# Low part of split weights in the second mixer: scaled ScalarE copy and an adding GpSimd transfer in place of a VectorE subtraction

## The chip, the cores and the metric

The kernel runs on one core of one Trainium2 chip. The metric is the device time of one execution in microseconds, the median of several runs. A profile is one execution of the same program, recorded by the hardware profiler.

## The reference

A trunk of two layers on a sequence of 256 tokens with 2048 features, all in float32. Each layer is a root-mean-square norm, a token mixer and a residual add, then a norm, a gated feed-forward block (5504 hidden features, a depthwise convolution of width 3 on the gate branch) and a residual add. The first layer's mixer is a bidirectional mLSTM with 8 heads. The second one's, which the change touches, is a bidirectional gated linear recurrence (HGRN2) with 16 heads of 128:

```python
p = hn @ w_in                       # 2048 -> 3*2048 + 2*2048
q, i, g, f_f, f_b = split(p)
k, log_f = gate(f)                  # for f_f and f_b; lower bound lb
y = hgrn_direction(q, k_f, lf_f, v) + flip(hgrn_direction(flip(q), flip(k_b), flip(lf_b), flip(v)))
y = head_rmsnorm(y, head_g, B_HEADS) * silu(g)
return y @ w_out
```

What the change touches is how the weights of `hn @ w_in` are prepared.

## The kernel before

**Big products.** All matrix products with weights are one stream. A Chunk is a block of output columns over all k-tiles of 128: kind "fm" (256 columns, features on the partitions), "tm" (512 columns, tokens on the partitions) or "one". `stream` takes the chunks in order and issues TensorE's matmuls (L181 to L183 for "tm", L188 and L189 for "fm").

**Split weights.** TensorE multiplies in the type float32r, which holds fewer bits than float32. `split_weights` therefore makes of each weight two float32r parts whose sum is the weight. SyncE loads up to 2048 columns (1 MiB) into a `raw` buffer (L133; three buffers, `RAW`). Then for each piece of 1024 columns ScalarE casts `raw` to the high part `wh` (L139), and VectorE subtracts `wh` from `raw` to give the low part `wl` (L140). `wh` and `wl` have four buffers each (`WB`), and `stream` fetches three pieces ahead of their use (`LOOK`). A "tm" piece is two k-tiles with 12 matmuls of 512 columns (high x high, high x low, low x high for two halves of the tokens). An "fm" piece is four k-tiles with 16 matmuls: for each of two blocks of features `wh` times both parts of x (512 columns), and `wl` times the high part (256 columns).

**The second mixer.** `hgrn` lays out its input products in four rounds, each for four heads: one "tm" chunk of `w_bv` (8 pieces), six "fm" chunks of `w_bq` (24 pieces; q, forward gate and backward gate of the heads), one "tm" chunk of `w_bg` (8 pieces). 160 pieces in all. When a chunk of `w_bq` is done, `take` evicts it (ScalarE copy L200, VectorE L201, L206), makes the gates (ScalarE L548, L549; VectorE L550, L551) and the products with q on GpSimd (L552, L554, L557). The head's own chain is then fed into the stream as side work: for seven levels, small matmuls `pd` (L590), VectorE products `QK` (L591, L592), copies `km` and `qm` (L574), masked copies into `AT` (L569), and GpSimd products `G` (L597). Matmuls `py` (L613) end it. The output projection `w_bout` follows, with the same split of its weights.

**The order.** The program text gives an order by `side.tick`, which counts assumed product time. A scheduler then fixes the order of instructions on each engine when the program is built. Each engine works through its own list in that order; GpSimd issues its transfers from the same list as its arithmetic, and SyncE issues the weight loads.

Of the kernel before, what the change touches and what calls it, by code (L numbers as in the profile page):

```python
# [8 lines left out]
F32 = mybir.dt.float32  # L9
F32R = mybir.dt.float32r  # L10
I32 = mybir.dt.int32
AF = mybir.ActivationFunctionType
ALU = mybir.AluOpType
# [3 lines left out]
T = 256  # L17
D = 2048
KT = D // P
# [21 lines left out]
LOOK = 3  # L41
# [9 lines left out]
def trunk_kernel(ctx, tc, xT, pp_d, cst_d, w_gate, w_aq, w_ak, w_av, w_ao, w_aout,  # L51
                 w_bq, w_bv, w_bg, w_bout, w_up, w_down, out, mscr, stop=9):
    nc = tc.nc
    act, dve, pool, pe = nc.scalar, nc.vector, nc.gpsimd, nc.tensor
# [13 lines left out]
    hT = [hx[:, k] for k in range(KT)]  # L68
# [6 lines left out]
    def aux(name):  # L75
        return psa.tile([P, 512], F32, tag="aux", name=name)

# [1 line left out]
    class Side:  # L79
        def __init__(self):  # L80
            self.now, self.jobs = 0.0, []
# [24 lines left out]

    side = Side()

# [1 line left out]
    class Chunk:  # L110
        def __init__(self, kind, src, nk, x, done, before=None, last=False):
            self.last = last
            self.kind, self.src, self.nk, self.x, self.done, self.before = kind, src, nk, x, done, before
            self.width = {"fm": 256, "tm": 512, "one": P}[kind]

    def split_weights(chunks):
        """raw -> the exact sum of two float32r parts, LOOK pieces ahead of their use"""
        first = True
        for ch in chunks:
            total = ch.nk * ch.width  # L120
            cuts = [0, 512, 1024] if first else [0]
            if ch.last and total % 1024:
                cuts.append(total % 1024)
            while cuts[-1] < total:
                cuts.append(min(total, cuts[-1] + (1024 if first else 2048)))
            for b0, b1 in zip(cuts, cuts[1:]):
                n = b1 - b0
                if first:
                    for k0, k1 in {0: [(0, 1)], 512: [(1, 2)], 1024: [(2, 4)], 2048: [(4, 8)], 4096: [(8, 12)],
                                   6144: [(12, 16)]}.get(b0, []):  # L130
                        nc.sync.dma_start(hx[:, k0:k1], xT[:, k0:k1])
                raw = wpool.tile([P, 2048], F32, tag="raw", bufs=RAW, name="raw")
                nc.sync.dma_start(raw[:, :n], ch.src[:, b0:b0 + n])  # L133
                for c0 in range(0, n, 1024):
                    m = min(1024, n - c0)
                    wh = wpool.tile([P, 1024], F32R, tag="wh", bufs=WB, name="wh")
                    wl = wpool.tile([P, 1024], F32R, tag="wl", bufs=WB, name="wl")
                    r = raw[:, c0:c0 + m]
                    act.copy(wh[:, :m], r)  # L139
                    dve.tensor_tensor(wl[:, :m], r, wh[:, :m].bitcast(F32), ALU.subtract)  # L140
                    yield wh, wl, m // ch.width
            first = False

    def stream(chunks):
        pieces = split_weights(chunks)
        ready = []

# [62 lines left out]
    def late(dst, src):  # L210
        tc.keep_in_program_order(nc.sync.dma_start(dst, src))

# [1 line left out]
    class Norm:  # L214
        def __init__(self, gname, goff, final=False, first=False):
            self.first = first
# [52 lines left out]
        return rs  # L269

    def project(wsrc, nk, x, norm):
        """hT += W^T x, 256 features at a time; the next norm takes each tile as it is done."""
        def done(c):
            def f_(ps):
                for f in range(2):
                    k = 2 * c + f
                    if norm is not None and norm.final and c == 7:
                        dve.tensor_tensor(hT[k], hT[k], ps[f][:, 0:T], ALU.add)
                        norm.add(k)
                        continue  # L280
                    b = ev.tile([P, T], F32, tag="b", bufs=3, name="b")
                    act.copy(b, ps[f][:, T:2 * T])
                    dve.tensor_tensor(hT[k], hT[k], ps[f][:, 0:T], ALU.add)
                    dve.tensor_tensor(hT[k], hT[k], b, ALU.add)  # L284
                    if norm is not None:
                        norm.add(k)
            return f_
        return [Chunk("fm", wsrc(c), nk, x, done(c), last=(norm is not None and norm.final and c == 7))
                for c in range(8)]
# [2 lines left out]
        where = keep if j < KT else more  # L292
        return where.tile([P, 2 * T], F32R, tag=f"yt{j}", name=f"{name}{j}")

# [1 line left out]
    def mlstm(norm, nxt):  # L296
        YT = [None] * KT
        H = 64
# [191 lines left out]
        def end():  # L490
            side.drain()
            stack.close()

        tail = project(lambda c: w_aout[c], KT, yx, nxt)
        tail[1].before = end
        return chunks + tail

# [1 line left out]
    def hgrn(norm, nxt):  # L499
        YT = [None] * KT  # L500
        stack = ExitStack()
# [118 lines left out]
        def finish(qd, four):  # L620
            for j in range(4):
                hd = 4 * qd + j
                while "y" not in heads[hd]:
                    yield
                y, rs = heads[hd]["y"]
                for t in range(2):
                    c = slice(t * P, (t + 1) * P)
                    dve.scalar_tensor_tensor(y[:, c], y[:, c], rs[:, t:t + 1], four["sg"][:, t, j * P:(j + 1) * P],
                                             ALU.mult, ALU.mult)
                yield  # L630
                pz = aux("pz")
                for t in range(2):
                    c = slice(t * P, (t + 1) * P)
                    pe.transpose(pz[:, c], y[:, c], ident)
                YT[hd] = slot(hd, "yb")
                split(YT[hd], pz[:, 0:T], col("b_head_g", hd))

        heads = [dict() for _ in range(BH)]
        chunks = []
        for qd in range(BH // 4):  # L640
            four = dict()

            def done_v(ps, four=four):
                four["V"] = box["mp"].tile([P, 2, 512], F32, tag="V", bufs=1, name="V")
                for t in range(2):
                    act.activation(four["V"][:, t], ps[t], AF.Copy, scale=norm.rc[:, t:t + 1])

            def done_g(ps, four=four, qd=qd):
                sg = four["sg"] = box["mp"].tile([P, 2, 512], F32, tag="sg", bufs=1, name="sg")
                for t in range(2):  # L650
                    act.activation(sg[:, t], ps[t], AF.Sigmoid, scale=norm.rc[:, t:t + 1])
                    dve.scalar_tensor_tensor(sg[:, t], ps[t], norm.rc[:, t:t + 1], sg[:, t], ALU.mult, ALU.mult)
                side.push(finish(qd, four))

            chunks.append(Chunk("tm", w_bv[qd], KT, norm.x, done_v, begin if qd == 0 else None))
            for i in range(6):
                def done_i(ps, i=i, qd=qd):
                    for f in range(2):
                        r = 2 * i + f
                        take(4 * qd + r // 3, r % 3, ps[f])  # L660
                chunks.append(Chunk("fm", w_bq[6 * qd + i], KT, norm.x, done_i))
            for j in range(4):
                heads[4 * qd + j]["qd"] = four
            chunks.append(Chunk("tm", w_bg[qd], KT, norm.x, done_g))

        def yx(k):
            side.until(lambda: YT[k] is not None)
# [2 lines left out]
        def end():  # L670
            side.drain()
            stack.close()

        tail = project(lambda c: w_bout[c], KT, yx, nxt)
        tail[1].before = end
        return chunks + tail

# [1 line left out]
    def ffn(layer, norm, nxt):  # L679
        stack = ExitStack()  # L680
        box = {}
# [25 lines left out]
        for part, (f0, nf) in enumerate(((0, FA), (FA, FB))):  # L707
            GT = []
            for i in range(nf):
                chunks.append(Chunk("fm", w_up[layer, f0 + i], KT, norm.x, done_up(f0 + i, i, GT),  # L710
                                    begin if f0 + i == 0 else None))
            chunks += project(lambda c: w_down[layer, c][:, f0 * 256:(f0 + nf) * 256], nf,
                              lambda k, GT=GT: GT[k], nxt if part else None)
        return chunks, stack.close

# [1 line left out]
    pool.memset(ones, 1.0)  # L717
    pool.memset(hmx, -0.5)
    pool.memset(pad, 0.0)
# [6 lines left out]
    chunks = mlstm(n0, n1)  # L726
# [17 lines left out]
    if stop > 3:  # L744
        order = ((0, pool), (2, dve), (3, dve), (1, pool), (4, dve), (5, dve), (6, dve), (7, dve))
        for n, (c, eng) in enumerate(order):
            r = (nf.R if eng is pool else nf.pr[:, 0:T]).unsqueeze(1).broadcast_to([P, 2, T])
# [8 lines left out]


def _cols(w, width):
    """[K, n*width] -> [n, 128, (K/128)*width]: a chunk of columns, its k-tiles side by side on each partition."""
    K, N = w.shape  # L760
    v = w.reshape(K // P, P, N // width, width).transpose(2, 1, 0, 3)
    return np.ascontiguousarray(v).reshape(N // width, P, (K // P) * width)


def _pcol(v):
    """[..., n*128] -> [128, ...*n]"""
    return np.asarray(v).reshape(-1, P).T


# [63 lines left out]
```

## Time and profile before

| | us |
|---|---|
| median of 3 runs | 2487.5 |
| lowest and highest run | 2486.99, 2487.65 |
| span of the profiled execution, first to last instruction | 2485.1 |
| busy in the span: TensorE matmul, VectorE, ScalarE, GpSimd | 2453.6, 1799.6, 1195.9, 311.0 |

For the profiled execution only its span is recorded; the runs' median lies 2.4 us above it. In the profile PE is TensorE's matmuls, PEld its weight loads, DVE VectorE, ACT ScalarE, POOL GpSimd, SP SyncE. L140 is line 140 of the kernel. A group's row gives line, engine, operation, output <- inputs, shapes and count, then busy us and mean ns of one, then the idle time of the engine just before these instructions and what ended it. A row of a DMA issue ends with KB of one and median us from issue to landing. "Landing" is when all of a transfer has arrived.

### The profile page before, as it was taken

Reading aid. Unit: us, or ns where it says so; the run is one execution under the profiler, and the core shown is the slowest. Engines: PE = TensorE matmul, PEld = TensorE weight load, DVE = VectorE, ACT = ScalarE, POOL = GpSimd, SP = SyncE. Lnnn points to the kernel's source line nnn. Section 1 sums busy time; section 2 is a strip of 40 time slices with the busy share of each in tenths; the row PEclk is TensorE's granted clock in tenths of the full one; section 3 lists DMA queues with packets and bytes.
Section 4 is the critical chain, followed back from the end, with each engine's and each line's share of the span. In section 5 each row is a group of like instructions: output and inputs, shape, how many; then the busy total and the mean of one; then the engine's idle time right before and its main releaser. Section 6 shows DMA issues by size and latency. Waiting matters only on the chain.

```text
span 2485.1 us, 35987 instructions
## 1 busy us (share of the span) xinstructions
PE 2453.6 (99%) x13934; PEld 2138.7 (86%) x13934; DVE 1799.6 (72%) x3001; ACT 1195.9 (48%) x1802; POOL 311.0 (13%) x368
## 2 busy tenths in 40 slices
PE   8999999999999999999999999999999999999998
PEld 6888888888888888888888888888888888888887
DVE  7766677777656777666979798897777765677754
ACT  5555455544444444444444444445544444444543
POOL 4100032000000000121404131324000000000022
PEclk9999999999999999999999999999999999999999
DMA  6654555555556555556454544545556555665553
GB/s 240 190 178 165 187 178 188 193 187 188 186 189 199 187 188 190 185 187 195 147 170 137 169 153 153 166 140 187 187 186 189 193 184 192 192 189 190 190 189 123
DMA packets 66204, 449.07 MB, mean 181 GB/s; under 512 B 7649, under 2 KB 8161, under 8 KB 15729
## 3 DMA queue, kind: packets, MB, share of 16 engines
q1 hardware_dynamic: 64656, 443.56, 54.8%
q0 software_dynamic: 800, 2.16, 0.6%
q8 instruction: 109, 1.79, 0.3%
q10 hardware_dynamic: 576, 1.05, 0.1%
q14 instruction: 63, 0.51, 0.1%
HBM read 444.58 MB, written 2.16 MB: 180 GB/s over the span
## 4 chain that ended last, share of the span: by engine, by line
PE 89%; DVE 8%; issue 2%; ACT 0%; DMA 0%; SPq 0%; DVEq 0%; POOL 0%; POOLq 0%
PE mm L188 49%; PE mm L189 25%; PE mm L182 4%; PE mm L183 4%; PE mm L181 4%; DVE wl L140 3%; DVE QK L591 1%; DVE AT L569 1%; PE pd L590 1%; DVE QK L592 1%; DVE qm L574 1%; DVE km L574 1%; PE pn L408 1%; PE mm L170 1%; PE py L613 0%
## 5 line engine op out<-in xcount | busy, mean ns | idle before, releaser
L140 DVE TENSOR_TENSOR wl<-raw,wh 128x1024 fp32r<-128x1024 f32 (+2 forms) x859 | 1051.8, 1225 | 550.2 <-ACT wh L139 536.9
L188 PE MATMUL mm<-xt,wh 128*128 128x512 f32 x3792 | 1324.5, 394 | 0.0
L139 ACT CAST wh<-raw 128x1024 fp32r<-128x1024 f32 (+2 forms) x859 | 884.2, 1030 | 857.8 <-PE mm L188 475.6
L189 PE MATMUL mm<-xt,wl 128*128 128x256 f32 x3792 | 1060.4, 280 | 0.0
L188 PEld LDWEIGHTS mm<-xt,wh 128*128 128x128 f32 x3792 | 710.7, 187 | 160.6
L189 PEld LDWEIGHTS mm<-xt,wl 128*128 128x128 f32 x3792 | 715.0, 189 | 0.4
L188 PE MATMUL mm<-g,wh 128*128 128x512 f32 x1334 | 462.6, 392 | 0.0
L189 PE MATMUL mm<-g,wl 128*128 128x256 f32 x1334 | 371.6, 279 | 0.0
L188 PEld LDWEIGHTS mm<-g,wh 128*128 128x128 f32 x1334 | 249.8, 187 | 56.3
L189 PEld LDWEIGHTS mm<-g,wl 128*128 128x128 f32 x1334 | 251.3, 188 | 0.0
L181 PE MATMUL mm<-wh,xt 128*128 128x512 f32 x512 | 203.3, 400 | 6.1 <-ACT wh L139 6.1
L182 PE MATMUL mm<-wl,xt 128*128 128x512 f32 x512 | 204.5, 399 | 4.6 <-DVE wl L140 4.6
L183 PE MATMUL mm<-wh,xt 128*128 128x512 f32 x512 | 202.7, 396 | 0.0
L200 ACT COPY b<-mm 128x256 f32<-128x256 f32 x237 | 87.6, 370 | 180.7 <-PE mm L189 180.7
L232 POOL TENSOR_TENSOR acc<-hx 128x256 f32<-128x256 f32 x5 | 5.4, 1085 | 1242.3 <-DVE hx L284 1239.9
L181 PEld LDWEIGHTS mm<-wh,xt 128*128 128x128 f32 x512 | 97.1, 190 | 26.8 <-ACT wh L139 7.1
L182 PEld LDWEIGHTS mm<-wl,xt 128*128 128x128 f32 x512 | 97.4, 190 | 24.3 <-DVE wl L140 5.9
L183 PEld LDWEIGHTS mm<-wh,xt 128*128 128x128 f32 x512 | 97.4, 190 | 19.5
L235 POOL TENSOR_TENSOR sq<-hx 128x256 f32<-128x256 f32 x65 | 71.7, 1114 | 198.0 <-DVE hx L284 195.5
L188 PE MATMUL mm<-yb,wh 128*128 128x512 f32 x256 | 90.6, 399 | 0.0
L188 PE MATMUL mm<-ya,wh 128*128 128x512 f32 x256 | 89.1, 394 | 0.0
L201 DVE TENSOR_TENSOR a<-mm,b 128x256 f32<-128x256 f32 x86 | 36.5, 424 | 51.0 <-ACT b L200 50.9
(175 smaller groups left out, 2093.2 us busy)
## 6 DMA issues: line engine op xcount, KB each, us to landing
raw<-in_w_up SPq DMA_DIRECT2D x172, 1024.0 KB, 5.1
raw<-in_w_down SPq DMA_DIRECT2D x64, 1024.0 KB, 4.9
raw<-in_w_bq SPq DMA_DIRECT2D x48, 1024.0 KB, 5.1
raw<-in_w_ao SPq DMA_DIRECT2D x16, 1024.0 KB, 4.9
raw<-in_w_aout SPq DMA_DIRECT2D x16, 1024.0 KB, 5.1
raw<-in_w_bv SPq DMA_DIRECT2D x16, 1024.0 KB, 4.9
raw<-in_w_bg SPq DMA_DIRECT2D x16, 1024.0 KB, 4.8
raw<-in_w_bout SPq DMA_DIRECT2D x16, 1024.0 KB, 5.1
```

The lines of the kernel that those rows point to most:

```text
L139: act.copy(wh[:, :m], r)
L140: dve.tensor_tensor(wl[:, :m], r, wh[:, :m].bitcast(F32), ALU.subtract)
L170: pe.matmul(ps[f][:, 0:T], w[:, c:c + P], x[:, o:o + T], start=(k + kk == 0 and i == 0), stop=(k + kk == ch.nk - 1 and i == 2))
L181: pe.matmul(ps[t], xh, wh[:, c], start=st, stop=False)
L182: pe.matmul(ps[t], xh, wl[:, c], start=False, stop=False)
L183: pe.matmul(ps[t], xl, wh[:, c], start=False, stop=sp)
L188: pe.matmul(ps[f], wh[:, c:c + P], x, start=st, stop=False)
L189: pe.matmul(ps[f][:, 0:T], wl[:, c:c + P], x[:, 0:T], start=False, stop=sp)
L200: act.copy(b, ps[:, T:2 * T])
L201: dve.tensor_tensor(dst, ps[:, 0:T], b, ALU.add)
L235: eng.tensor_tensor(s, hT[k], hT[k], ALU.mult)
L574: dve.tensor_copy(m.rearrange("k (m p j) -> k m p j", p=2, j=h), blocks(z, h, 0, T))
```

## The change

For the chunks of `w_bv`, `w_bq` and `w_bg` (marked `summed`), and only for these, the low part is made in another way. ScalarE copies `raw` a second time, with scale -1, into the float32r buffer `wl`, which then holds the negated high part. GpSimd then issues a transfer that reads the same weights once more from HBM and adds them onto `wl`. The sum is the low part. The VectorE subtraction of these 160 pieces is gone. All other weights keep the subtraction. Line numbers from L143 on are four higher in the changed kernel.

```diff
     class Chunk:
-        def __init__(self, kind, src, nk, x, done, before=None, last=False):
-            self.last = last
+        def __init__(self, kind, src, nk, x, done, before=None, last=False, summed=False):
+            self.last, self.summed = last, summed
...
                     act.copy(wh[:, :m], r)
-                    dve.tensor_tensor(wl[:, :m], r, wh[:, :m].bitcast(F32), ALU.subtract)
+                    if ch.summed:
+                        act.activation(wl[:, :m], r, AF.Copy, scale=-1.0)
+                        pool.dma_start(wl[:, :m], ch.src[:, b0 + c0:b0 + c0 + m], accum_op=ALU.add)
+                    else:
+                        dve.tensor_tensor(wl[:, :m], r, wh[:, :m].bitcast(F32), ALU.subtract)
...
-            chunks.append(Chunk("tm", w_bv[qd], KT, norm.x, done_v, begin if qd == 0 else None))
+            chunks.append(Chunk("tm", w_bv[qd], KT, norm.x, done_v, begin if qd == 0 else None, summed=True))
...
-                chunks.append(Chunk("fm", w_bq[6 * qd + i], KT, norm.x, done_i))
+                chunks.append(Chunk("fm", w_bq[6 * qd + i], KT, norm.x, done_i, summed=True))
...
-            chunks.append(Chunk("tm", w_bg[qd], KT, norm.x, done_g))
+            chunks.append(Chunk("tm", w_bg[qd], KT, norm.x, done_g, summed=True))
```

## The prediction

> **What bounds the kernel now.** I read the page first (busy time, chain), then cut the second mixer's input stage into its period and asked for the busy time, the groups and the waits of that stretch.
>
> ```profile
> span 2485.1 us, 35987 instructions
> ...
> PE 2453.6 (99%) x13934; PEld 2138.7 (86%) x13934; DVE 1799.6 (72%) x3001; ACT 1195.9 (48%) x1802; POOL 311.0 (13%) x368
> ...
> PE 89%; DVE 8%; issue 2%; ACT 0%; DMA 0%; SPq 0%; DVEq 0%; POOL 0%; POOLq 0%
> ```
>
> Over the whole span TensorE is the bound: 99% busy, 89% of the chain. VectorE has 8% of the chain. Where the changed pieces are multiplied shows a row of the view of the tile wl, asked for 1107 to 1648 us (durations, first and last start):
>
> ```profile
> L182 PE MATMUL mm<-wl,xt x247: 388/389/486, 1122.6 to 1647.6; 128*128 128x512 f32 x124
> ```
>
> The w_bv and w_bg products on L182 open and close the stage: 1122.6 to 1647.6, 525 us. It is four rounds of 40 pieces (a piece is 1024 columns, 512 KB of weights: 8 for w_bv, 24 for w_bq, 8 for w_bg). Three of the rounds by the view of busy time in given stretches (stretch, length, then busy us of PE, PEld, DVE, ACT and POOL, granted clock, DMA share, GB/s), then a stretch of the first feed-forward stage:
>
> ```profile
> 1198.65:1333.83 135.18, 132.77 (x761) 115.13 (x760) 117.79 (x243) 59.94 (x100) 37.16 (x48) 1.00 0.48 156
> 1333.83:1469.04 135.21, 132.83 (x761) 115.19 (x761) 118.00 (x243) 59.97 (x100) 35.76 (x48) 1.00 0.48 156
> 1469.04:1604.18 135.14, 132.72 (x761) 115.15 (x760) 117.77 (x244) 59.96 (x100) 37.16 (x48) 1.00 0.48 156
> ```
>
> ```profile
> 700.00:1000.00 300.00, 300.00 (x1732) 264.50 (x1732) 203.02 (x310) 142.15 (x200) 0.00 (x0) 1.00 0.59 191
> ```
>
> The reader is to see that a round lasts 135.2 us, so a piece takes 135.2/40 = 3.38 us (3.28 over the 160 of the whole stage, since the first round starts without head work), and that TensorE is idle for only 135.18 - 132.77 = 2.4 us of it although VectorE is at 118 of 135 us. In the same round, the chain by line, one row of its pieces (start, us), the groups of the two engines that make the parts, and the waits (us, times, longest):
>
> ```profile
> by line: DVE wl L140 15.2%; PE mm L188 12.0%; issue 10.0%; DVE QK L591 7.0%; PE mm L182 6.3%; PE mm L181 6.3%; PE mm L183 6.2%; PE mm L189 5.9%; DVE QK L592 5.5%; DVE qm L574 4.6%; DVE AT L569 4.5%; DVE km L574 4.5%; PE pd L590 2.2%; DVE G
> ...
> 1255.12 1.34 PE pd L590 x12
> ```
>
> ```profile
> L140 DVE TENSOR_TENSOR wl<-raw,wh 128x1024 fp32r<-128x1024 f32 x41 | 51.8, 1263 | 14.2 <-ACT wh L139 13.9
> ```
>
> ```profile
> L139 ACT CAST wh<-raw 128x1024 fp32r<-128x1024 f32 x40 | 42.0, 1050 | 32.6 <-PE mm L188 15.0 <-PE mm L183 14.8 <-DVE QK L591 1.2
> ...
> L651 ACT ACTIVATE sg<-mm,rc 128x512 f32<-128x512 f32 x2 | 1.4, 691 | 1.0 <-PE mm L183 1.0
> ```
>
> ```profile
> ACT wh L139 <- PE mm L188: 15.0, 11, 1.8
> ACT wh L139 <- PE mm L183: 14.8, 9, 3.4
> DVE wl L140 <- ACT wh L139: 13.9, 12, 2.1
> ```
>
> Here the subtraction L140 is the largest item of the chain (15.2%), with the heads' VectorE work around it. TensorE and VectorE take turns as the limit. The cast on ScalarE waits mostly for TensorE: it starts when a buffer comes free, so the pipeline already runs at the depth of its four buffers.
>
> **How much there is to win.** The feed-forward stretch has no head work: 1732 matmul rows in 300.0 us, 16 rows a piece, is 300/(1732/16) = 2.77 us a piece. Forty such pieces are 110.8 us. A round has 761 rows, of which 24 x 16 + 16 x 12 = 576 are products; the other 185 belong to the heads, at 1.34/12 = 0.11 us each 20.4 us. TensorE's own work is then 131.2 us of 135.2: 4 us a round, 16 us in four rounds, is all that a free VectorE can give.
>
> **The change part by part.** 160 pieces change (4 x 40). *Removed*: 160 subtractions of 1.26 us on VectorE, 50.5 us a round; VectorE falls to about 67 of 135 us and leaves the chain. By itself: at most -16 us. *ScalarE*: one copy with scale more per piece. The trace has none of that shape. From below it is the cast, 1.05 us; from above 691 ns for 512 columns twice, 1.38 us. I take 1.1, since the cast has the same operands. ScalarE goes from 59.9 to 59.9 + 40 x 1.1 = 104 us of 135: not the bound, but wh and wl of a piece now stand one behind the other, 2.15 us.
>
> *GpSimd*: 160 issues more, each of which waits for ScalarE's copy, and GpSimd takes its work in order. Behind the waiting issue stand the heads' G products (L597), QK products (L552), the copy L554 and the memset L566. VectorE's L591 and L592 wait for G, and TensorE's pd (L590) for those. The issue's own price, and the only transfers that GpSimd makes now:
>
> ```profile
> L380 POOL DMA_DIRECT2D Mb<-mscr x16: 536/546/585, 67.0 to 160.4; - x16
> ...
> DMA to landing us min/median/max: 3.8/5.1/7.2
> ```
>
> Forty issues of 0.55 us are 22 us a round on top of 37: GpSimd has room, 59 of 135. The new order puts the G products one or two between two issues, so a piece that lands late also holds up a head by as much; I count that inside the piece time below, as both follow the same buffer.
>
> *The transfers.* Each adds 512 KB from HBM onto the old content of wl. The rows:
>
> ```profile
> q1 hardware_dynamic: 64656, 443.56, 54.8%
> q0 software_dynamic: 800, 2.16, 0.6%
> ...
> raw<-in_w_bq SPq DMA_DIRECT2D x48, 1024.0 KB, 5.1
> ...
> Mb<-mscr POOLq DMA_DIRECT2D x16, 128.0 KB, 5.1
> ...
> raw<-in_w_down SPq DMA_DIRECT2D x1, 512.0 KB, 3.5
> ```
>
> ```profile
> GB/s 351 150 0 126 384 89 0 206 393 5 0 0 206 393 9 0 103 393 103 0 0 267 332 0 0 178 407 14 9 37 262 300 0 89 384 131 0 0 70 295
> ```
>
> The last row is from the DMA view of 1330 to 1400 us, in slices of 1.75 us: with work queued the 16 engines reach 407 GB/s, so 512 KB (524,288 bytes) passes in 1.29 us. By the share of the first row, 443.56 MB in 54.8% of 2485.1 us is 326 GB/s, 1.61 us. An adding transfer must fetch the old wl as well as the weights before it writes. I found no transfer of that kind in the trace, so its price is bounded: one pass from below (1.29 us, the read of wl costs nothing), two passes of the slow kind from above. That slow kind is q0, the software queue: 2.16 MB in 0.6% of the span, 14.9 us, is 145 GB/s, 3.6 us a pass, 7.2 for two. I take two passes at the speed of the weight loads, because these rows are 4 KB like theirs and the q0 rows are 1 KB.
>
> So a piece now asks the DMA engines for its plain load and two passes more. At 407 GB/s that is 3 x 1.29 = 3.87 us, at 326 GB/s 3 x 1.61 = 4.83 us, and both are over the 3.38 us that a piece takes today. **The DMA engines become the bound of this stage.** With a full queue the 407 is the nearer row; the queue runs empty at times, because a transfer can't start before its buffer is free. I take 4.15 us. By the Trainium skill, Collectives: The Full Stack, section "The bandwidth ceiling: the fold count and why AG ≠ RS ≠ AR", a reducing transfer runs at about half the rate of a copy since it reads two sources, 32.35 against 62.28 GB/s; by that ratio a piece would ask for 1.29 + 1.93 x 1.29 = 3.78 us and the sum would be 2567 us. No run here shows it yet.
>
> *The loop of four buffers.* wl of piece i can be rewritten when TensorE has done with piece i-4, and TensorE wants it three pieces later. In those three piece times must fit: two ScalarE copies 2.15, the issue 0.55, and the time to landing L. With 3 x 3.38 = 10.1 us, L may be 7.4 us before it costs anything. From below L is 3.5 us (512 KB on SyncE's queue), hidden. From GpSimd's queue, 128 KB took 5.1 us; 384 KB more (0.97) and a second pass (1.29) make 7.4, just the cover; with the longest, 7.2, L is 9.5 and a piece (2.7 + 9.5)/3 = 4.05 us. The loop thus has no reserve either, and full DMA engines lengthen L: that is why I stay above 3.87. By the Trainium skill, DMA: Bandwidth & Descriptors, section "Anatomy of one DMA — SWDGE (gpsimd) path", a GpSimd transfer takes 2.0 us plus its bytes at 436 GB/s. That would be 3.2 us for 512 KB and would hide wholly. The trace's Mb row disagrees: 5.1 us for 128 KB, where this rule gives 2.3.
>
> *The rest.* The stages outside keep their instructions; the first pieces are fetched under the end of the feed-forward stage, which moves a few us at most. Sum: the stage goes from 525 to 160 x 4.15 = 664 us, so the span to 2485.1 + 139 = 2624 us. The runs' median, 2487.5, lies 2.4 us above the profiled span, so **2627 us**.
>
> **The rivals.**
> 1. *Faster.* The adding transfer occupies the engines under 3.38 - 1.29 = 2.09 us and lands within 7.4 us. Then VectorE's relief comes through: 2487.5 - 16 = 2472 us. For it: DMA is only 0.48 busy in this stage, and VectorE leads the chain. Against it: two passes (2.58) are already over that point, and only one pass fits.
> 2. *A slow adder.* If the adding queue runs like q0, one pass is 3.6 us and a piece 3.6 + 1.29 = 4.9 us, the stage 784: 2747 us. With two passes 7.2 + 1.61 = 8.8 us, the stage 1408: 3370 us. For it: the only software-queue rows are that slow. Against it: their rows are a quarter as long.
> 3. *Only the loop decides.* The engines keep up but L is 7.4 to 9.5 us: from no loss, 2488 us, to 4.05 us a piece, 2611 us; in the middle 3.6, 2539 us. For it: Mb's 5.1 us. Against it: it needs the cheap pass together with the long landing.
> 4. *Nothing to see*: the relief of VectorE and a small loss cancel, 2483 to 2492 us.
>
> **How the numbers follow.** The forecast, 3.87 to 4.83 us a piece, 2582 to 2735 us: 0.5. Slow adder: 0.2. Loop alone: 0.1. Faster: 0.15. No change: 0.05. About 0.2% (5 us) is what a measurement of this kernel can tell from no change. Faster 0.15, same 0.05, slower 0.80. The range runs from 2470, the full relief, to 2830, a piece of 5.4 us; it leaves out the larger part of the slow adder and hardly anything below.
>
> **What would show it.** In the new profile: rounds of about 166 us instead of 135; DMA share in them near 0.9 or more, not 0.48; TensorE idle some 30 us a round, ended by the landing of wl; VectorE near 67 us and gone from the chain. Loop alone would show the same idle time with a DMA share under 0.8. The slow adder would show wl landings over 12 us. The forecast is wrong if the landings stay under 7.4 us and rounds are shorter than 135 us.

## The result, and the profile after

The changed kernel takes 2563.6 us, the median of 4 runs (2561.58 to 2569.76); the kernel before took 2487.24 us beside it. The ratio is 1.0311, 95% interval 1.0298 to 1.0324: 76 us slower. The profiled execution is the run of 2569.76 us. First lines of its page, and its DMA queues (packets, MB, share of 16 engines):

```profile
span 2568.0 us, 36293 instructions
...
PE 2481.5 (97%) x13934; PEld 2144.6 (84%) x13934; DVE 1646.5 (64%) x2841; ACT 1346.4 (52%) x1962; POOL 408.2 (16%) x528
...
q1 hardware_dynamic: 64656, 443.56, 51.1%
q0 software_dynamic: 23840, 86.06, 17.2%
...
PE 81%; DMA 12%; issue 4%; POOL 2%; ACT 1%; DVE 1%; SPq 0%; DVEq 0%; POOLq 0%; ACTq 0%
```

VectorE fell from 8% of the chain to 1%, and DMA came in with 12%. The stage's ends show best where the output projection (tile yb) begins. Before, then after, the second row of "after" being the first use of wl in the stage:

```profile
L188 PE MATMUL mm<-yb,wh x256: 389/398/481, 1659.4 to 1754.0; 128*128 128x512 f32 x128
```

```profile
L192 PE MATMUL mm<-yb,wh x256: 390/392/477, 1746.0 to 1836.7; 128*128 128x512 f32 x128
```

```profile
L186 PE MATMUL mm<-wl,xt x256: 387/393/628, 1125.3 to 1745.5; 128*128 128x512 f32 x128
```

The stage goes from 1122.6-1659.4, 537 us, to 1125.3-1746.0, 621 us: 84 us more. It starts 2.7 us later, and the projection behind it takes 91 us in place of 95. The sum is the 83 us between the spans. One round after the change, in the columns used above, and the same stretch in the view of DMA queues and issues:

```profile
1319.40:1471.87 152.47, 138.00 (x760) 113.63 (x759) 79.48 (x202) 97.18 (x140) 60.35 (x89) 1.00 1.05 275
```

```profile
DMA  9999999999999999999999999999999999999999
...
q0 software_dynamic: 5732, 20.86, 69.6%
q1 hardware_dynamic: 2873, 20.92, 34.9%
...
wl<-in_w_bq POOLq DMA_DIRECT2D x25, 512.0 KB, 10.0
raw<-in_w_bq SPq DMA_DIRECT2D x12, 1024.0 KB, 9.0
```

The reader is to see four things. The round is 152.5 us, 17 more than before. VectorE is down from 118 to 79 us. The DMA share went from 0.48 to 1.05 (packets of the two queues overlap, hence over 1), and the row of tenths shows 0.9 or more in each of 40 slices. And the plain weight loads, which nobody changed, now land after 9.0 us where they took 5.1.

The two queue rows give the price of the unknown operation. q0: 69.6% of 152.5 us for 20.86 MB is 2.67 us for 512 KB. q1: 34.9% for 20.92 MB is 1.33 us for 512 KB. **In this round an adding transfer keeps the DMA engines busy twice as long as a plain load of the same bytes.** Together 4.0 us of engine time a piece, done in 3.81 (152.5/40) thanks to the overlap. The price of a plain load isn't fixed: before the change 512 KB took 1.61 us (47.3% of the 440 us from 1200 on, 67.95 MB). So a ratio holds only within one stretch.

The waits in the same round, of the copy into wl and of TensorE's weight loads, then those of its matmuls, then the chain:

```profile
ACT wl L141 <- PE mm L186: 15.2, 13, 2.5
...
PEld mm L193 <- DMA wl<-in_w_bq: 13.0, 12, 1.8
```

```profile
PE mm L193 <- DMA wl<-in_w_bq: 9.6, 12, 1.4
PE mm L186 <- DMA wl<-in_w_bv: 3.4, 6, 0.8
PE mm L186 <- DMA wl<-in_w_bg: 1.5, 2, 0.9
```

```profile
by line: DMA wl<-in_w_bq 39.3%; issue 18.7%; DMA wl<-in_w_bg 13.8%; DMA wl<-in_w_bv 7.2%; PE mm L192 5.1%; POOL wl L142 4.6%; PE mm L193 3.8%; ACT wl L141 2.7%; PE pd L594 2.0%; PE mm L186 1.9%; POOL rs L272 1.5%; POOL QK L556 1.5%; PE mm L
```

TensorE waits for landings of wl: the three rows make up all of its 14.5 idle us (152.47 - 138.00), and 60% of the round's chain are these landings. ScalarE waits for TensorE to free wl. Such a ring of waits can't tell by itself whether the slow part is the engines' throughput or the length of the ring. That is what the experiments are for.

### The profile page after: what moved, and what is told of

Read it like the earlier page. It is cut to its first block, busy times and chain, and to the rows that moved or that the text cites. A ratio compares the mean times of both kernels' runs of the same rounds, so it can differ in the third digit from the quotient of the medians.

```text
span 2568.0 us, 36293 instructions
## 1 busy us (share of the span) xinstructions
PE 2481.5 (97%) x13934; PEld 2144.6 (84%) x13934; DVE 1646.5 (64%) x2841; ACT 1346.4 (52%) x1962; POOL 408.2 (16%) x528
## 3 DMA queue, kind: packets, MB, share of 16 engines
q10 hardware_dynamic: 576, 1.05, 0.1%
## 4 chain that ended last, share of the span: by engine, by line
PE 81%; DMA 12%; issue 4%; POOL 2%; ACT 1%; DVE 1%; SPq 0%; DVEq 0%; POOLq 0%; ACTq 0%
PE mm L192 45%; PE mm L193 24%; DMA wl<-in_w_bq 7%; DMA wl<-in_w_bg 3%; PE mm L186 3%; PE mm L187 3%; PE mm L185 3%; DMA wl<-in_w_bv 2%; POOL wl L142 1%; PE pd L594 1%; PE pn L412 1%; ACT wl L141 1%; PE mm L174 1%; PE py L617 0%; DVE xt L200 0%
## 5 line engine op out<-in xcount | busy, mean ns | idle before, releaser
L144 DVE TENSOR_TENSOR wl<-raw,wh 128x1024 fp32r<-128x1024 f32 (+2 forms) x699 | 849.6, 1216 | 497.2 <-ACT wh L139 485.0
L141 ACT ACTIVATE wl<-raw 128x1024 fp32r<-128x1024 f32 x160 | 169.2, 1057 | 62.8 <-PE mm L186 62.4
L142 POOL DMA_DIRECT2D wl<-in_w_bq x96 | 85.0, 887 | 224.5 <-ACT wl L141 145.6
```

What stands on the lines that cost most here:

```text
L141: act.activation(wl[:, :m], r, AF.Copy, scale=-1.0)
L142: pool.dma_start(wl[:, :m], ch.src[:, b0 + c0:b0 + c0 + m], accum_op=ALU.add)
```

## The experiments

Three theories. **A:** the throughput of the DMA engines bounds the stage. **B:** the loop of four buffers bounds it: copy, issue, landing in a row take longer than three pieces of products. **C:** the software queue is slow whatever it carries. The times of the kernel before, in the three groups of runs, were 2487.72, 2487.59 and 2487.39 us.

**The relief alone.** The adding transfer is taken out; wl then holds only the negated high part.

```diff
                         act.activation(wl[:, :m], r, AF.Copy, scale=-1.0)
-                        pool.dma_start(wl[:, :m], ch.src[:, b0 + c0:b0 + c0 + m], accum_op=ALU.add)
```

> The changed kernel without the adding transfers: wl holds the negated high part only (the addition is left out). It shows what VectorE's relief with ScalarE's second copy is worth by itself. Theory A and B: VectorE at about 67 to 80 us of a round, the relief is at most 16 us, time 2471 to 2480 us. If ScalarE's two copies in a row were part of the loss, it would stay above 2487 us.

2472.53 us, ratio 0.9939 (0.9923 to 0.9956), 15 us faster. A round:

```profile
1277.90:1409.60 131.70, 131.70 (x762) 115.12 (x760) 74.07 (x202) 97.44 (x141) 27.29 (x48) 1.00 0.49 160
```

TensorE is busy for all of 131.7 us. ScalarE's double work (97 us) costs nothing. So everything that the change loses, 91 us against this run, comes with the transfers: their engine time, their issues, the waits for them.

**Plain in place of adding.**

```diff
-                        pool.dma_start(wl[:, :m], ch.src[:, b0 + c0:b0 + c0 + m], accum_op=ALU.add)
+                        pool.dma_start(wl[:, :m], ch.src[:, b0 + c0:b0 + c0 + m])
```

> The changed kernel with the adding taken out: GpSimd's 160 transfers are plain copies of the same weights into wl (the low part is then wrong; this leaves out the addition). Same issues, same waits, same bytes from HBM. Theory A (the 16 DMA engines are the bound, an adding transfer costs two passes): a piece asks for 1.36 + 1.36 = 2.7 us instead of 1.36 + 2.65 = 4.0, under the 3.36 us that it takes without the change, so the stage falls from 621 us to 537 or less, time 2470 to 2490 us, DMA share well under 1. Theory B (the loop of four buffers is the bound: copy, issue, landing in a row): the landing shortens by one pass only, 1.3 us in three pieces, stage 552 us or more, time about 2500 us. Theory C (the software queue is slow in itself, whatever it carries): still about 2564 us.

2492.94 us, ratio 1.0023 (1.0014 to 1.0033). A round, and the landings of these transfers (min/median/max):

```profile
1283.90:1421.60 137.70, 134.56 (x762) 116.30 (x761) 75.77 (x202) 97.22 (x141) 48.11 (x88) 0.99 0.89 308
```

```profile
DMA to landing us min/median/max: 3.8/6.0/9.1
```

As many transfers, the same waits and the same HBM bytes without the second pass: 71 us of the loss are gone. C falls. One thing more changed with it: a plain issue takes GpSimd 0.54 us, an adding one 0.88. A piece's transfer now takes 1.58 us of engine time beside 1.45 for a load (46.7% for 71.35 MB and 42.9% for 71.49 MB, of the 460 us from 1140 on). The loads have rows of 8 KB, these transfers of 4 KB; queue and rows together thus cost a tenth, and the rest of the doubling is the adding. But A asked for 2490 at most, and 20 us against the relief alone remain although the engines are no longer full.

**Half of the columns of each piece.**

```diff
-                        pool.dma_start(wl[:, :m], ch.src[:, b0 + c0:b0 + c0 + m], accum_op=ALU.add)
+                        pool.dma_start(wl[:, :m // 2], ch.src[:, b0 + c0:b0 + c0 + m // 2], accum_op=ALU.add)
```

> The changed kernel, but each adding transfer covers only the first 512 of a piece's 1024 columns (the low part of the other half is left wrong). Every piece still goes through copy, issue, landing. Theory A: a piece asks the DMA engines for 1.36 + 1.33 = 2.7 us, no longer the bound, time 2470 to 2490 us. Theory B: the fixed part of the landing and the chain ahead of it stay, the loss falls by less than half, about 2530 us.

2504.89 us, ratio 1.0069 (1.0054 to 1.0084): between the two theories, over A's 2490 and under B's 2530. A round takes 137.6 us with a DMA share of 0.91. Its issues take 0.88 us like those of the change, so the dearer issue can hardly explain more than the 12 us between this run and the plain one.

**Every second piece.**

```diff
-                    if ch.summed:
+                    if ch.summed and c0:
```

> The changed kernel with only every second piece (the second of each 1 MiB load) made by ScalarE and the adding transfer, the first by the VectorE subtraction; nothing is left out. Theory A: 1.36 + 2.65/2 = 2.7 us of DMA engine time a piece, not the bound; VectorE is relieved of half, 25 us a round; time 2474 to 2485 us, faster than the kernel before. Theory B: half of the pieces still pay, about 2520 us.

2508.3 us, ratio 1.0086 (1.0071 to 1.0101). It fails A's expectation, which was faster than before; B's 2520 is nearer. The landings:

```profile
DMA to landing us min/median/max: 5.3/7.9/10.2
```

With half of the load and with all of it, different things seem to rule. The next runs are to part them.

**The load without the loop.** The kernel before, with plain copies whose data nobody waits for.

```diff
                 nc.sync.dma_start(raw[:, :n], ch.src[:, b0:b0 + n])
+                if ch.summed:
+                    late(dscr[turn[0] % 8], ch.src[:, 0:4096])
+                    turn[0] += 1
```

> The kernel before (VectorE subtraction, no adding transfer), but SyncE issues behind each 1 MiB weight load of the second mixer's input products a plain copy of 2 MiB from HBM to an HBM scratch that nobody reads: the DMA engines get as many bytes to pass as the two passes of two adding transfers, and no piece waits for them. Theory A (the DMA engines' throughput bounds the changed stage): the stage goes from 537 to 610 us or more, time 2560 us or more. Theory B (the loop of copy, issue and landing bounds it): about 2488 us, as before.

2615.25 us, ratio 1.0513 (1.0497 to 1.0529). A round of it:

```profile
1318.00:1481.60 163.60, 141.14 (x760) 116.41 (x760) 117.07 (x243) 58.30 (x101) 29.76 (x48) 0.99 0.99 383
```

VectorE still subtracts and no adding transfer is in the way, and the stage is slower than with the change. The weight loads stand behind the copies in SyncE's queue: those of w_bq landed after a median of 18.6 us in place of 5.1, so here the loop of the `raw` buffers grew. But with a DMA share of 0.99 the engines have no time left: engine load alone is enough.

**Finer pieces, all adding.** Pieces of 512 columns with eight buffers, seven ahead, in the same memory.

```diff
-LOOK = 3
+LOOK = 7
-WB = 4
+WB = 8
...
-                for c0 in range(0, n, 1024):
-                    m = min(1024, n - c0)
-                    wh = wpool.tile([P, 1024], F32R, tag="wh", bufs=WB, name="wh")
-                    wl = wpool.tile([P, 1024], F32R, tag="wl", bufs=WB, name="wl")
+                for c0 in range(0, n, 512):
+                    m = min(512, n - c0)
+                    wh = wpool.tile([P, 512], F32R, tag="wh", bufs=WB, name="wh")
+                    wl = wpool.tile([P, 512], F32R, tag="wl", bufs=WB, name="wl")
```

> The changed kernel with pieces of 512 columns in place of 1024 (eight buffers of half the size, seven pieces ahead), in all stages; nothing is left out. In the same memory the cover of the chain grows: seven half pieces are 11.5 us less one copy pair 1.2 and one issue 0.9, 9.4 us, instead of 9.8 - 2.15 - 0.9 = 6.8 us. Theory A: the bytes stay, so the stage stays at 610 to 640 us; the time stays at 2560 us or above. Theory B: the stage falls to 540 us or less, time near that of the kernel before with the same pieces.

2568.94 us, ratio 1.0325 (1.0310 to 1.0341). A round:

```profile
1310.90:1465.30 154.40, 136.96 (x760) 114.21 (x760) 82.57 (x202) 107.81 (x222) 97.45 (x128) 1.00 1.09 273
```

With all the bytes, a longer cover (the time from a buffer's coming free to its next use, less ScalarE's two copies) changes nothing. The landings, of half the bytes each, took a median of 11.7 us, where the same 256 KB took 6.7 in the run with half of the columns: they follow the load of the engines. One reservation: the halved rows take somewhat more engine time by the byte (DMA share 1.09 against 1.05), so a small gain of the loop could hide behind it, not one of 80 us.

**The control for finer pieces**: the kernel before with the same cut.

> The kernel before with pieces of 512 columns in all stages, the control for the two runs with fine pieces. More and shorter instructions on ScalarE and VectorE, no other work: both theories 2485 to 2510 us.

2492.03 us, ratio 1.0018 (1.0009 to 1.0028).

**Finer pieces, every second adding.** The cut above and

```diff
-                    if ch.summed:
+                    if ch.summed and c0 % 1024:
```

> As the run with pieces of 512 columns, but only every second of them is made by the adding transfer; nothing is left out. Half the adding bytes left a loss of about 35 us against the relief alone when the pieces had 1024 columns. If that rest is the loop of buffers (landings of 5.3 to 10.2 us against a cover of 6.8), the cover of 9.4 us takes most of it: 2475 to 2490 us, or 5 to 15 us under the kernel before with the same pieces. If it is the DMA engines' throughput after all, it stays at about 2508 us.

2496.82 us, ratio 1.0037 (1.0023 to 1.0051): 5 us over its control, where the same bytes in coarse pieces stood 21 us over theirs. So with half the load the cover did matter, as B has it. I had expected a win over its control, and there was none. A landing is counted from the start of its issue (in the changed kernel's chain, the landing of 10.34 us from 1319.71 us begins where that issue begins), so the issue must not come off the cover again as it does in the expectation: 11.5 - 1.2 = 10.3 us stand against a median of 7.9 and a longest of 12.8. Cover and size of the transfers changed together here; which of the two brought the 16 us isn't parted.

**One piece in four.**

```diff
-                    if ch.summed:
+                    if ch.summed and c0 and b0 % 4096 == 0:
```

> The changed kernel with one piece in four made by the adding transfer, the others by the subtraction; nothing is left out. Every second piece left 21 us over the kernel before. DMA engine time 1.36 + 0.66 = 2.0 us a piece; VectorE relieved by 12.6 us a round, worth up to 4 us in all. If bursts on the DMA engines make the landings late (theory A with the loop of buffers), fewer adding transfers in a row leave 2485 to 2495 us. If each adding transfer costs a fixed wait, half of the 21 + 8 us: about 2498 us.

2503.59 us, ratio 1.0070 (1.0054 to 1.0087), hardly less than with every second piece. A round, then the landings:

```profile
1291.30:1429.20 137.90, 133.08 (x762) 115.08 (x761) 108.21 (x232) 69.77 (x111) 39.98 (x58) 1.00 0.68 191
```

```profile
DMA to landing us min/median/max: 5.4/8.1/9.3
```

The engines have a third of their time free, and still the landing takes 8.1 us against a cover of 3 x 3.28 - 2.15 = 7.7 us. Here B rules: a typical adding transfer is late by 0.4 us. TensorE's waits for these landings in the whole stage (us, times, longest):

```profile
PE mm L193 <- DMA wl<-in_w_bq: 15.3, 12, 2.0
PE mm L186 <- DMA wl<-in_w_bv: 5.4, 2, 4.9
...
PE mm L186 <- DMA wl<-in_w_bg: 0.6, 1, 0.6
```

That is 21 us in 15 waits for 40 transfers, and the relief of a quarter doesn't pay for it. By engine time an adding transfer costs 2.89 us here and a load 1.62 (21.2% for 17.67 MB, 47.7% for 71.18 MB, of 460 us), a ratio of 1.8.

**Source in SBUF.**

```diff
-                        pool.dma_start(wl[:, :m], ch.src[:, b0 + c0:b0 + c0 + m], accum_op=ALU.add)
+                        pool.dma_start(wl[:, :m], r, accum_op=ALU.add)
```

> The changed kernel, but the adding transfer takes the weights from the raw buffer in SBUF instead of a second time from HBM; nothing is left out. The raw buffer is held until the transfer has landed. Theory A (passes of the DMA engines, whatever the source): two passes remain, stage 610 to 650 us, time 2555 us or more, more if the held raw buffers delay the loads. Rival: the second read of HBM is the price; then the HBM traffic of the stage is as before the change and the time falls under 2520 us.

2600.97 us, ratio 1.0452 (1.0437 to 1.0468). A round lasts 162.5 us with a DMA share of 1.03, and over the 460 us from 1140 on q0 takes 67.5% where q1 takes 35.8% for the same bytes, 1.9 times as much. The second read of HBM isn't the price. That it is even slower than the change fits the raw buffers, which are held longer, but that wasn't tried apart.

**What TensorE waited for.** GpSimd works through its list in order, so an issue that waits for ScalarE also holds up the heads' products behind it. That would be a rival for what remains at part load. The traces answer it: for each run, the median landing and TensorE's matmul waits for landings of wl in the whole stage. The first column is against the kernel before; with 512 columns, against the control.

| GpSimd's transfers | time, us | DMA share of a round | median landing, us | waits for landings, us |
|---|---|---|---|---|
| adding, all pieces (the change) | +76 | 1.05 | 10.3 | 62 |
| adding, source in SBUF | +114 | 1.03 | 9.2 | 77 |
| adding, all, 512 columns | +77 | 1.09 | 11.7 | 63 |
| adding, every second | +21 | 0.87 | 7.9 | 24 |
| adding, half of the columns | +17 | 0.91 | 6.7 | 19 |
| adding, one in four | +16 | 0.68 | 8.1 | 21 |
| adding, every second, 512 columns | +5 | 0.92 | 7.9 | 7 |
| plain, all pieces | +5 | 0.89 | 6.0 | 12 |
| none (relief alone) | -15 | 0.49 | none | 0 |

All other waits of TensorE's matmuls in the stage come to 7 us at most in these runs, and to 10 in the kernel before. So the loss is in the landings, not in heads that GpSimd holds up. A late issue would show as a late landing too; but with one piece in four GpSimd waited ahead of its issues almost only for ScalarE's copy (167 of 168 us). For the change, 62 of the 91 us are such waits; the rest stands in matmul time (138 against 131.7 us a round), whose ends the profile models.

**VectorE relieved without a transfer.** Since the relief was worth 15 us, I moved other VectorE work of this stage to ScalarE, in the kernel before: the copies km and qm.

```diff
-                dve.tensor_copy(m.rearrange("k (m p j) -> k m p j", p=2, j=h), blocks(z, h, 0, T))
+                act.copy(m.rearrange("k (m p j) -> k m p j", p=2, j=h), blocks(z, h, 0, T))
```

> The kernel before with the heads' copies km and qm (56 a round of 0.36 us, 20 us) on ScalarE in place of VectorE; nothing is left out and no transfer is added. The relief alone measured 15 us for 50 us a round less on VectorE. If VectorE's load is what counts, 20 us a round less gives 5 to 10 us: 2478 to 2483 us. If the copies stand behind ScalarE's casts, which wait for buffers, the heads come late and it is slower: 2490 to 2510 us.

2474.02 us, ratio 0.9946 (0.9931 to 0.9961): **faster than both kernels**, 13 us under the kernel before. A round, with all of TensorE's time in use:

```profile
1277.40:1409.20 131.80, 131.80 (x762) 115.21 (x761) 105.73 (x186) 79.84 (x157) 35.65 (x48) 1.00 0.49 160
```

With km alone on ScalarE:

> As the run before it, but only km (28 a round, 10 us) on ScalarE. If VectorE's load counts, 3 to 5 us: 2482 to 2485 us. If the wait behind ScalarE's casts counts, 2488 to 2500 us.

2476.93 us, ratio 0.9957 (0.9942 to 0.9972). Both runs gained more than I expected: 10 us a round of copies taken from VectorE gave 10 us of time, 20 us gave 13. VectorE's busy time fell by less, from 118 to 106 us with both copies: L591 and L592 took longer beside them (521 and 551 ns against 481 and 462).

A deeper loop with pieces of 1024 columns was not tried.

## Why the prediction was right, and where its sizes were off

- *The mechanism*: right. The DMA engines became the bound of the stage, at the share over 0.9 that was named as its sign; the loop alone was to show a share under 0.8. The time by itself would not have told: 2563.6 us lies under the 2582 to 2735 us that stood beside the forecast's chance and inside the 2488 to 2611 of the rival in which only the loop decides.
- *TensorE's own 131.2 us a round, and 16 us as all that VectorE's relief can give*: right. 131.7 us and 15 us in the run with the relief alone.
- *VectorE at 67 us*: it was 79, and 74 with the relief alone. The sum of its rows fell by 50 us as forecast (136 to 86 with the relief alone), but instructions overlap on VectorE: 136 us of rows were 118 us busy before. It left the chain all the same.
- *ScalarE, 1.1 us a copy, hidden*: right. 1.06 us, and no loss in the run with the relief alone. *GpSimd's issue, 0.55 us* from the Mb row: it was 0.88 us. The plain run's 0.54 for the same bytes shows that the adding makes the difference, not the size. GpSimd still was busy for only 60 of 152 us.
- *Two passes at the speed of the weight loads*: right. 2.67 against 1.33 us in the round, 1.8 to 2.0 times as much over the runs with rows of 4 KB, and up to 2.2 with rows of 2 KB. The reason that I gave, rows of 4 KB like the loads', was wrong, as the loads' rows are 8 KB (1 MiB over 128 rows); the plain run shows that it mattered little. The slow adder, at 3.6 us a pass, is refuted (its sign, landings over 12 us, was met by the longest of 13.9 but not by the median of 10.3), and so is the faster rival, whose point was 2.09 us. The ratio 2.0 lies near the 1.93 that the Trainium skill gives for reducing against copying in ring collectives (Collectives: The Full Stack, section "The bandwidth ceiling: the fold count and why AG ≠ RS ≠ AR"). The sum by that ratio, 2567 us, came nearer than mine, but by luck: with the stage's true 537 us before, it gives 2555.
- *4.15 us a piece*: the term that was most off in size, and with it the rounds of 166 us and the 30 us of idle TensorE (152.5 and 14.5). The stage gave 621/160 = 3.88 us. I had added 0.28 us to the lower bound of 3.87 for a queue that runs empty at times; the engines were at 0.9 or more in every slice of the round. That is 43 us of the 63 between 2627 and 2564. That 3.87 was met so closely is partly luck: the engine time was 4.0 us a piece, and overlap brought it to 3.81 in a round.
- *A stage of 525 us before*: wrong by 12 us. I had read its end from a view cut at 1648 us, and the last products on L182 lay beyond. The yb row puts it at 1659.4. The rest is small: the projection's 4 us, and a profiled run that was the slowest of the four.
- *The loop*: it had little reserve, as I said, but I counted the issue twice, since a landing is measured from the issue's start. By my own terms the cover was 10.1 - 2.15 = 8.0 us, not 7.4. With only one piece in four the landing of 8.1 us lay between my 7.4 and 9.5. By the rule of the Trainium skill (DMA: Bandwidth & Descriptors, section "Anatomy of one DMA — SWDGE (gpsimd) path") the estimate is 3.2 us; no landing of an adding transfer of 512 KB was under 5.2 us here.
- What I hadn't seen is that the loop costs something even at a load that the engines can carry: with all pieces adding it is masked by the throughput, with fewer it is what remains. The engines' throughput is the cause of the result; late landings are why neither half nor a quarter of the same change paid. Why a landing takes 8 us with the engines a third free stays open.

## What to carry to other kernels

A transfer that adds onto SBUF cost the DMA engines about two plain ones of the same bytes here (1.8 to 2.2): price it against the DMA share of the stage that it goes into, not of the whole span, and add the plain loads. Then check the landing against the buffers' cover, because a stage may have room for the bytes and still not for the wait. And before buying relief for an engine with transfers, look for work of the same stage that an idle engine can take: 20 us a round of small copies gave 13 us, nearly the 15 of 50 us of subtractions.

## What the runs showed of the hardware that I had not expected

- Plain loads of 1 MiB on SyncE's queue went from 5.1 to 9.0 us to landing beside a full software queue. Their engine time fell meanwhile, from 1.61 to 1.33 us for 512 KB.
- An adding issue of 512 KB takes GpSimd 0.88 us, a plain one 0.54.
- One adding transfer in four pieces, with the engines busy for 0.68 of the time, still took a median of 8.1 us to land; a plain one of the same size took 6.0 at a share of 0.89. Of the 2.1 us between them 0.34 is the longer issue; the other 1.8 are more than the 1.3 us of engine time by which the two differ (2.89 and 1.58).
